# Two slabs of the gate's u moved in front of the opening norm, and the second block's opening norm moved two steps later

## The chip, the cores and the metric

The kernel runs on one core of one Trainium2 chip. The metric is the device time of one execution in microseconds (us), as the median of several runs. TensorE (PE) multiplies matrices into PSUM; VectorE (DVE), ScalarE (ACT) and GpSimd (POOL) do the elementwise work; SyncE (SP) issues most of the DMAs. In the rows of the profile, PEld is TensorE's loading of weights.

## What is computed

Two transformer blocks stand one behind the other over one sequence of 512 tokens and 1024 features. The change touches the mixer of the first block and the entry into the second. Cut to that, the reference is:

```
# first block
a = rmsnorm(h, ln_pre_mix)
q, k, v, u, z = split(a @ w_in)
attn = dilated_attention(q, k, v)
u, z = gelu(u), gelu(z)                       # the spatial gate, 4 groups of 128 features
z = layernorm(z, ln_g, ln_b)                  # within each group
sgu = u * (einsum('gij,bnjgc->bnigc', wm, zc) + b_s)
h = h + rmsnorm(concat(rmsnorm(attn), rmsnorm(sgu)) @ w_out)
...                                           # feed-forward, then a sigmoid gate on h
# second block
h = rms_norm(x, norm_mix) * (1 + sc1) + sh1
q, k, v = split(h @ w_in)                     # stick-breaking attention
...
```

A norm here is a factor per token (one over the root of the mean square) and a gain per feature. The kernel puts the gain into the operand in advance and the factor on the product behind it, so that a projection can start before the norm's factor is known.

## The kernel before, in words

Activations are kept feature by token: eight tiles `X` of 128 features by 512 tokens. Every product of two fp32 numbers is made of three passes: each operand is split into a high part (`whi`, `hh`, cast by ACT) and the rest (`wlo`, `hl`, subtracted by DVE), and `mm3` (line 95 issues every matmul) runs low weights, high weights, and high weights with the low activations. A **slab** is 128 output features by 512 tokens: 8 steps over the features times 3 passes, 24 matmuls of 128x512 into one PSUM bank. `tokmajor` makes a product token by feature instead, in four banks at once: 96 matmuls. One `unit` (line 101) loads 512 KB of weights on SP's queue and splits them into two pairs `whi`, `wlo`; there are four buffers for raw weights and seven each for `whi` and `wlo`, so a cast waits until TensorE is through with the pair seven places back.

PSUM has three banks `mm`, two banks `sc`, one bank `po` and a pair `tt`.

A norm over the features has two halves. `norm_cols` (line 235) multiplies the summed squares by a column of ones on TensorE (rows `tt<-ones1k,acc`), DVE adds epsilon (`ms`, line 241) and GpSimd takes the power -1/2 (`rc`, line 243). `norm_rows` (line 246) spreads `rc` over all partitions by TensorE (rows `tt<-ident,rc`), and DVE copies the result to `R` (line 258). `stats` is one behind the other. The sum of squares is made by ACT (`sq`, line 209) and added up on GpSimd or DVE (`acc`, line 204).

`mixer_a` (line 354) opens the first block. The product for z comes first, token by feature, in the three `mm` banks and `po`; then `stats` gives `rc0` and `R0`; then the product for v takes the same four banks, which the four gelus of z (line 403, scaled by `rc0`) must have left. The shift of the gate (`RB`, line 419, from eight small matmuls `sc<-wmT,lnb` and `sc<-bsr,onesr`) and the layer norm of z follow. Then, for each of the four groups, one slab for u, its product with `R0` on DVE, its gelu on ACT, four small matmuls `sc<-wmT,z` and the gating.

`enter` (line 848) opens each half of the second block's layers, with `b` from 0 to 3: four slabs (two `mm` banks, one `sc`, `po`) run over the unnormed activations `xd`, step by step over the features, each step 12 matmuls in the four banks. Between the steps stand the norm's columns and, one step later, its rows. Behind it `operand` (lines 879 to 881) makes the eight normed activations out of `R`, and `slab` (line 863) puts `R` on the four products, which frees their banks. After `enter(b=0)`, `mixer_sb` runs the product for v, token by feature, in the three `mm` banks and one `sc`.

The order in which instructions stand on an engine is not that of the code: the tile framework's scheduler sets it when the kernel is built. On an engine each instruction waits for the one before it.

Of the kernel before, what the change touches and what calls it, by code (L numbers as in the profile page):

```python
# [8 lines left out]
F32 = mybir.dt.float32  # L9
F32R = mybir.dt.float32r  # L10
BF16 = mybir.dt.bfloat16
AF = mybir.ActivationFunctionType
# [3 lines left out]
P = 128  # L16
S = 512
NB = S // P
D = 1024
KD = D // P  # L20
# [45 lines left out]
class K:  # L66
# [287 lines left out]
    def mixer_a(self, X, raw):  # L354
        tc, nc, a = self.tc, self.nc, self.a
        xs = []
# [7 lines left out]
        with ExitStack() as ctx:  # L364
            mp = ctx.enter_context(self.homes("mixa", [f"m{p}{i}" for p in "hl" for i in range(8)]))
            gctx = ctx.enter_context(ExitStack())
            pm2 = gctx.enter_context(tc.tile_pool(name="gate", bufs=1))
            w0 = a["w_in"]
# [9 lines left out]
            acc = None  # L378
            for k in range(KD):
                acc = self.add_square(acc, X[k])  # L380
            rc0, R0 = self.stats(acc, self.ones1k)

            pv = self.four()
            self.tokmajor(pv, [w0[8 + i] for i in range(4)], xs)
# [40 lines left out]

            sacc, ms = None, [None] * 8
            for g in range(4):
                pu = self.mm_ps()
                self.slabs([pu], [self.unit(w0[4 + g])], xs)
                u = self.t(pm2, [P, S], F32, "u", bufs=2)  # L430
                nc.vector.tensor_mul(u, pu, R0)
                nc.scalar.activation(u, u, AF.Gelu_apprx_tanh)
                pmx = self.sc_ps()
                for tb in range(NB):
                    self.matmul(pmx[:, tb * P:(tb + 1) * P], zt[tb][:, g * P:(g + 1) * P], wmT[:, g, :],
                                     start=True, stop=True)
                m = self.t(pm2, [P, S], F32, "m", bufs=2)
                nc.vector.scalar_tensor_tensor(m.rearrange("p (b i) -> p b i", b=NB),
                                               pmx.rearrange("p (b i) -> p b i", b=NB), self.col("sgu_ln_g"),
                                               RB[:, g:g + 1, :].to_broadcast([P, NB, P]), op0=ALU.mult, op1=ALU.add)  # L440
                nc.vector.tensor_mul(u, u, m)
                ms[4 + g] = self.split_scaled(u, self.col("sgu_out_norm", g), 4 + g, "m", mp)
                sacc = self.add_square(sacc, u, mp, "sacc")
# [7 lines left out]
            aacc, ks = [None], {}  # L451
# [66 lines left out]
            pss = []  # L518
# [329 lines left out]
    def enter(self, X, b, ws):  # L848

        nc = self.nc
        pss = [self.bank("mm"), self.bank("mm"), self.bank("sc"), self.bank("po")]
        w = self.units(ws)
        self.slabs(pss, w, self.xd, ks=range(0, 2))
        rc = self.norm_cols(self.acc, self.ones1k)
        self.slabs(pss, w, self.xd, ks=range(2, 3))
        R = self.norm_rows(rc)
        self.slabs(pss, w, self.xd, ks=range(3, KD))

        def slab(i, out=None, raw=False):
            u = self.t(self.sp, [P, S], F32, "sq", bufs=2) if out is None else out
            nc.vector.tensor_mul(u, pss[i], R)
            if raw:
                return u, self.bsh[b][:, i:i + 1]
            nc.scalar.activation(u, u, AF.Identity, bias=self.bsh[b][:, i:i + 1])
            return u

        mod, sh = self.mod[b // 2], 24 * (b % 2)

        def operand(pool, tag):

            xs = []
            for k in range(KD):
                hi = self.t(self.xp, [P, S], F32R, f"hh{k}", bufs=1)
                lo = self.t(self.xp, [P, S], F32R, f"hl{k}", bufs=1)
                f = self.t(pool, [P, S], F32, tag(k), bufs=1)
                shift = mod[:, sh + k:sh + k + 1]
                nc.vector.scalar_tensor_tensor(f, X[k], self.A[b][:, k:k + 1], R, op0=ALU.mult, op1=ALU.mult)  # L879
                nc.scalar.activation(hi, f, AF.Identity, bias=shift)  # L880
                nc.vector.scalar_tensor_tensor(lo, f, shift, hi.bitcast(F32), op0=ALU.add, op1=ALU.subtract)  # L881
                xs.append((hi, lo))
            return xs

        return slab, operand
# [522 lines left out]
```

## Time and profile before

| | |
|---|---|
| median of 3 runs | 1922.7 us (1921.9 to 1925.36) |
| the profiled execution's own time | 1926.12 us |
| its span, first to last instruction | 1924.4 us |
| TensorE busy | 1877.1 us, 98% of the span |
| VectorE, ScalarE, GpSimd busy | 1289.8, 897.7, 372.8 us |
| mean granted TensorE clock | 0.987 of full speed |

The times of runs are taken without the profiler; all views below are of the one profiled execution. Times in them count from the start of its span. A granted clock of 1.00 is 2.4 GHz, one of 0.50 is 1.2 GHz.

### The profile page before, as it was taken

How to read it: one execution, taken by the hardware profiler on the slowest of the kernel's cores; microseconds unless marked ns; L12 is line 12 of the kernel's file. 1: busy time of each engine (PE TensorE's matmuls, PEld its weight loads, DVE VectorE, ACT ScalarE, POOL GpSimd, SP SyncE). 2: the span in 40 equal slices, each digit the busy share in tenths (PEclk: the TensorE clock that was granted, in tenths of full speed). 3: DMA queues.
4: the chain of work that ended last, by engine and by line, in shares of the span. 5: the costliest groups of instructions: out<-in, count | busy, mean ns of one | idle time of the engine just before them, and what ended most of it. 6: DMA issues, size and time to landing. Idle time of an engine off the chain costs nothing.

```text
span 1924.4 us, 24081 instructions
## 1 busy us (share of the span) xinstructions
PE 1877.1 (98%) x8610; PEld 1508.7 (78%) x8610; DVE 1289.8 (67%) x2354; ACT 897.7 (47%) x1664; POOL 372.8 (19%) x348
## 2 busy tenths in 40 slices
PE   7999799999999999999999999999999999999999
PEld 5887678888887787777888888887666788888887
DVE  7686775556446666886878875568977677666431
ACT  5365433323323555554544443336489755444321
POOL 3020431111000302332111110003454211111000
PEclk8999899999999999999999999999999999999999
DMA  5232155555464233222266554633222123223331
GB/s 184 88 90 88 44 165 186 192 189 175 153 210 164 88 120 90 78 64 81 99 215 198 188 186 151 208 122 104 72 72 67 35 99 117 91 99 96 96 114 45
DMA packets 70382, 236.93 MB, mean 123 GB/s; under 512 B 8086, under 2 KB 8678, under 8 KB 70263
## 3 DMA queue, kind: packets, MB, share of 16 engines
q1 hardware_dynamic: 69556, 234.47, 37.8%
q8 instruction: 67, 1.10, 0.2%
q10 hardware_dynamic: 578, 0.85, 0.1%
q14 instruction: 53, 0.43, 0.1%
q0 software_dynamic: 128, 0.08, 0.0%
HBM read 226.87 MB, written 2.21 MB: 119 GB/s over the span
## 4 chain that ended last, share of the span: by engine, by line
PE 77%; DVE 6%; issue 2%; ACT 1%; POOL 0%; POOLq 0%; DVEq 0%; ACTq 0%
PE mm L95 45%; PE sc L95 26%; PE po L95 3%; PE tt L98 2%; PE tt L95 1%; DVE isc L1123 1%; DVE m L1122 1%; DVE hl L276 0%; DVE g L768 0%; DVE hl L881 0%; DVE v L1060 0%; DVE rst L223 0%; DVE isc L1103 0%; DVE q L879 0%; DVE wlo L113 0%
## 5 line engine op out<-in xcount | busy, mean ns | idle before, releaser
L113 DVE TENSOR_TENSOR wlo<-raw,whi 128x512 fp32r<-128x512 f32 (+1 forms) x518 | 381.1, 744 | 203.6 <-ACT whi L112 199.0
L112 ACT CAST whi<-raw 128x512 fp32r<-128x512 f32 (+1 forms) x550 | 326.8, 607 | 405.7 <-PE mm L95 236.4
L95 PE MATMUL mm<-hh,wlo 128*128 128x512 f32 (+1 forms) x1000 | 406.4, 406 | 3.5 <-ACT hh L275 3.5
L95 PE MATMUL mm<-hl,whi 128*128 128x512 f32 x1032 | 401.2, 392 | 0.0
L95 PE MATMUL mm<-hh,whi 128*128 128x512 f32 (+1 forms) x1000 | 392.0, 392 | 0.0
L95 PEld LDWEIGHTS mm<-hl,whi 128*128 128x128 f32 x1032 | 194.5, 188 | 42.3
L95 PEld LDWEIGHTS mm<-hh,wlo 128*128 128x128 f32 (+1 forms) x1000 | 189.3, 189 | 47.9 <-issue 8.5
L796 DVE CUSTOM_DVE_ANT_0 ada<-ada,bc 128x1024 f32<-128x1024 f32 x112 | 138.2, 1234 | 127.6 <-DMA ada<-in_ada_w 101.4
L95 PEld LDWEIGHTS mm<-hh,whi 128*128 128x128 f32 (+1 forms) x1000 | 189.1, 189 | 36.8 <-issue 1.1
L204 POOL TENSOR_TENSOR acc<-acc,sq 128x512 f32<-128x512 f32 x53 | 89.5, 1688 | 394.8 <-ACT sq L209 387.2
L95 PE MATMUL sc<-hh,wlo 128*128 128x512 f32 x416 | 162.8, 391 | 0.0
L95 PE MATMUL sc<-hl,whi 128*128 128x512 f32 x416 | 162.6, 391 | 0.0
L95 PE MATMUL sc<-hh,whi 128*128 128x512 f32 x416 | 162.5, 391 | 0.0
L95 PE MATMUL mm<-Hh,wlo 128*128 128x512 f32 x364 | 143.3, 394 | 0.0
L95 PE MATMUL mm<-Hh,whi 128*128 128x512 f32 x364 | 143.0, 393 | 0.0
L95 PE MATMUL mm<-Hl,whi 128*128 128x512 f32 x364 | 143.0, 393 | 0.0
L1034 POOL TENSOR_TENSOR g<-g,u 128x512 f32<-128x512 f32 x44 | 62.8, 1428 | 413.1 <-DVE u L1030 341.4
L266 ACT CAST Hh<-g 128x512 fp32r<-128x512 f32 x66 | 41.0, 622 | 164.2 <-POOL g L720 101.4
L95 PEld LDWEIGHTS sc<-hh,wlo 128*128 128x128 f32 x416 | 78.7, 189 | 16.3
L95 PEld LDWEIGHTS sc<-hl,whi 128*128 128x128 f32 x416 | 78.5, 189 | 16.5
L95 PEld LDWEIGHTS sc<-hh,whi 128*128 128x128 f32 x416 | 78.6, 189 | 16.3
L95 PE MATMUL sc<-Hh,wlo 128*128 128x512 f32 x220 | 86.7, 394 | 0.0
(370 smaller groups left out, 3328.8 us busy)
## 6 DMA issues: line engine op xcount, KB each, us to landing
ada<-in_ada_w SPq DMA_DIRECT2D x96, 512.0 KB, 3.9
raw<-in_ffn_w_up SPq DMA_DIRECT2D x88, 512.0 KB, 3.3
raw<-in_w_gate_up SPq DMA_DIRECT2D x44, 512.0 KB, 4.2
raw<-in_ffn_w_down SPq DMA_DIRECT2D x32, 512.0 KB, 3.6
raw<-in_sb_w_in SPq DMA_DIRECT2D x24, 512.0 KB, 3.2
raw<-in_dsa_w_in SPq DMA_DIRECT2D x21, 512.0 KB, 3.4
raw<-in_w_in SPq DMA_DIRECT2D x19, 512.0 KB, 3.3
raw<-in_w_down SPq DMA_DIRECT2D x16, 512.0 KB, 4.3
```

Of the source, the lines that this page charges most:

```text
L95: self.queue(self.nc.tensor.matmul(*args, **kw))
L98: self.queue(self.nc.tensor.transpose(*args))
L112: nc.scalar.copy(hi[:, :w], raw[:, c:c + w])
L113: (eng or nc.vector).tensor_sub(lo[:, :w], raw[:, c:c + w], hi[:, :w].bitcast(F32))
L204: (eng or self.nc.gpsimd).tensor_add(acc, acc, self.square(src))
L266: self.nc.scalar.copy(hi, src)
L796: nc.vector.tensor_tensor_reduce(raw, raw, row, scale=1.0, scalar=0.0, op0=ALU.mult, op1=ALU.add, accum_out=out))
L1034: nc.gpsimd.tensor_mul(g, g, u)
L1122: nc.vector.max(m8, work[qb][:, :L])
L1123: nc.vector.match_replace(work[qb][:, :L], m8, work[qb][:, :L], SENT)
```

## The change

In `mixer_a` the slabs of the first two groups of u are multiplied right behind z, into the two `sc` banks. The norm's columns come behind the first of the two slabs, the norm's rows behind the second. The product with `R0` and the gelu of these two groups follow at once, in front of v; the loop over the groups makes only the slabs of groups 2 and 3. In `enter`, for `b` = 0, the columns come behind the fourth step in place of the second, and the rows behind the fifth in place of the third; for `b` = 1 to 3 nothing changes. No instruction is added or removed on any engine.

```diff
@@ mixer_a
             for k in range(KD):
                 acc = self.add_square(acc, X[k])
-            rc0, R0 = self.stats(acc, self.ones1k)
+
+            pus = []
+            for g in range(2):
+                pus.append(self.sc_ps())
+                self.slabs(pus[-1:], [self.unit(w0[4 + g])], xs)
+                if g == 0:
+                    rc0 = self.norm_cols(acc, self.ones1k)
+            R0 = self.norm_rows(rc0)
+            us = []
+
+            def gated(g, pu):
+                u = self.t(pm2, [P, S], F32, "u", bufs=2)
+                nc.vector.tensor_mul(u, pu, R0)
+                nc.scalar.activation(u, u, AF.Gelu_apprx_tanh)
+                us.append(u)
+
+            for g in range(2):
+                gated(g, pus[g])
 
             pv = self.four()
             self.tokmajor(pv, [w0[8 + i] for i in range(4)], xs)
@@
             for g in range(4):
-                pu = self.mm_ps()
-                self.slabs([pu], [self.unit(w0[4 + g])], xs)
-                u = self.t(pm2, [P, S], F32, "u", bufs=2)
-                nc.vector.tensor_mul(u, pu, R0)
-                nc.scalar.activation(u, u, AF.Gelu_apprx_tanh)
+                if g > 1:
+                    pu = self.mm_ps()
+                    self.slabs([pu], [self.unit(w0[4 + g])], xs)
+                    gated(g, pu)
+                u = us[g]
                 pmx = self.sc_ps()
@@ enter
         w = self.units(ws)
-        self.slabs(pss, w, self.xd, ks=range(0, 2))
+        k = 2 if b else 4
+        self.slabs(pss, w, self.xd, ks=range(0, k))
         rc = self.norm_cols(self.acc, self.ones1k)
-        self.slabs(pss, w, self.xd, ks=range(2, 3))
+        self.slabs(pss, w, self.xd, ks=range(k, k + 1))
         R = self.norm_rows(rc)
-        self.slabs(pss, w, self.xd, ks=range(3, KD))
+        self.slabs(pss, w, self.xd, ks=range(k + 1, KD))
```

How the order on the engines moves, at three places. First TensorE behind the product for z (the last matmul into `po`), before and then with the change; a row with x4 is four matmuls.

```order
L95 MATMUL po_133<-wlo_274,hh_64_290 128x512
L95 MATMUL tt_334<-ones1k_101,acc_311 128x1 x4
L95 MATMUL sc_580<-wmT_498,lnb_505 128x128
L95 MATMUL sc_580<-bsr_501,onesr_503 128x128
L95 MATMUL tt_343<-ident_96,rc_341 128x128 x4
...
L95 MATMUL mm_350<-whi_356,hl_32_135 128x512
```

```order
L95 MATMUL po_133<-wlo_274,hh_64_290 128x512
L95 MATMUL sc_334<-hh_31_134,wlo_338 128x512
...
L95 MATMUL tt_369<-ones1k_101,acc_311 128x1 x4
L95 MATMUL sc_378<-hh_31_134,wlo_382 128x512
...
L95 MATMUL tt_413<-ident_96,rc_376 128x128 x4
L95 MATMUL mm_426<-whi_432,hl_32_135 128x512
```

A slab of 24 matmuls now stands in front of the columns (`tt_369`), another between them and the rows (`tt_413`), and v (`mm_426`) follows the rows directly; the eight small matmuls for `RB` stand behind v.

Second, VectorE in the same stretch, before and then with the change (`lbase` and `lt` belong to the attention's bias, made early; the `wlo` are those of v, and with the change they are v's first five).

```order
L643 TENSOR_TENSOR lbase_837<-lbase_837,lt_194_838 128x512
L113 TENSOR_TENSOR wlo_425<-raw_422,whi_424 128x512
L113 TENSOR_TENSOR wlo_429<-raw_422,whi_428 128x512
L241 TENSOR_SCALAR ms_339<-tt_334 128x4
L113 TENSOR_TENSOR wlo_459<-raw_456,whi_458 128x512
L258 COPY R_348<-tt_343 128x512
```

```order
L660 TENSOR_TENSOR lbase_837<-lbase_837,lt_194_838 128x512
L113 TENSOR_TENSOR wlo_433<-raw_430,whi_432 128x512
L113 TENSOR_TENSOR wlo_437<-raw_430,whi_436 128x512
L113 TENSOR_TENSOR wlo_467<-raw_464,whi_466 128x512
L113 TENSOR_TENSOR wlo_471<-raw_464,whi_470 128x512
L241 TENSOR_SCALAR ms_374<-tt_369 128x4
L113 TENSOR_TENSOR wlo_501<-raw_498,whi_500 128x512
```

`ms` now stands behind four subtractions of v's weights in place of two.

Third, VectorE in `enter(b=0)`, before and then with the change (`hl_1330` and `acc` end the first block; `mh` and `hl` are `operand`'s, `wlo_5694` the last weights of the four slabs).

```order
L204 TENSOR_TENSOR acc_5426<-acc_5426,sq_5642 128x512
L241 TENSOR_SCALAR ms_5726<-tt_5721 128x4
L258 COPY R_5747<-tt_5742 128x512
L879 SCALAR_TENSOR_TENSOR mh_1373_5828<-X_1_81,A_19_113,R_5747 128x512
L137 TENSOR_TENSOR wlo_5694<-raw_5663,whi_5693 128x512
```

```order
L204 TENSOR_TENSOR acc_5426<-acc_5426,sq_5642 128x512
L137 TENSOR_TENSOR wlo_5694<-raw_5663,whi_5693 128x512
L113 TENSOR_TENSOR wlo_5915<-raw_5912,whi_5914 128x512
L113 TENSOR_TENSOR wlo_5919<-raw_5912,whi_5918 128x512
L241 TENSOR_SCALAR ms_5750<-tt_5745 128x4
L113 TENSOR_TENSOR wlo_5949<-raw_5946,whi_5948 128x512
L258 COPY R_5771<-tt_5766 128x512
L897 SCALAR_TENSOR_TENSOR mh_1373_5828<-X_1_81,A_19_113,R_5771 128x512
```

Three subtractions of weights have come in front of `ms`, one between `ms` and `R`. Behind `R`, 15 of the 16 operations of `operand` still stand in front of the first product that frees a bank (`sq<-mm`). On TensorE v's first matmuls are reordered for it: 15 matmuls into the free banks `mm_5908` and `sc_5911` come before the first into `mm_5909`, where before there were three.

## Rows read from the trace of the kernel before

**Rows 1.** The page, busy us (share of the span) and instructions per engine.

```profile
PE 1877.1 (98%) x8610; PEld 1508.7 (78%) x8610; DVE 1289.8 (67%) x2354; ACT 897.7 (47%) x1664; POOL 372.8 (19%) x348
```

**Rows 2.** Waits of TensorE: who for whom, us in total, times, longest us.

```profile
PE tt L95 <- POOL rc L243: 9.4, 4, 5.2
PE tt L95 <- DVE acc L204: 8.7, 3, 5.4
```

**Rows 3.** Timeline of TensorE, opening norm: start us, us, form, xcount, idle before.

```profile
31.58 0.95 PE L95 MATMUL tt<-ones1k,acc 128*128 128x1 f32 x8
32.39 0.47 PE L95 MATMUL sc<-wmT,lnb 128*128 128x128 f32 x2
32.78 0.48 PE L95 MATMUL sc<-bsr,onesr 1*128 1x128 f32 x2
38.45 2.07 PE L95 MATMUL tt<-ident,rc 128*128 128x128 f32 x8 [5.18 <-POOL rc L243]
40.31 0.63 PE L95 MATMUL sc<-wmT,lnb 128*128 128x128 f32 x2
...
44.49 0.80 PE L95 MATMUL mm<-whi,hl 128*128 128x512 f32 x1
...
48.34 0.40 PE L95 MATMUL po<-whi,hl 128*128 128x512 f32 x1
```

**Rows 4.** Windows: stretch, its us, busy us (instructions) per engine, PEclk, DMA.

```profile
38.50:48.30 9.80, 9.80 (x29) 7.68 (x30) 4.19 (x27) 2.93 (x5) 0.00 (x0) 0.51 0.10 38
```

**Rows 5.** The chain that ended last, in order of time, a piece at full clock.

```profile
264.17 10.88 PE mm L95 x48
```

**Rows 6.** Timeline of DVE, POOL and ACT, opening norm.

```profile
35.12 1.70 DVE L113 TENSOR_TENSOR wlo<-raw,whi 128x512 fp32r<-128x512 f32 x2
...
36.98 1.41 POOL L243 TENSOR_TENSOR rc<-ms,mhalf 128x4 f32<-128x4 f32 x1 [0.70 <-DVE ms L241]
...
32.19 1.28 ACT L403 ACT_TABLE_LOAD   x1
38.43 1.84 ACT L403 ACTIVATE z<-mm,rc 128x512 f32<-128x512 f32 x3 [4.96 <-POOL rc L243]
```

**Rows 7.** DMA issues of the page: xcount, KB each, median us to landing.

```profile
raw<-in_w_in SPq DMA_DIRECT2D x19, 512.0 KB, 3.3
```

**Rows 8.** Timeline of TensorE, the second block's opening norm.

```profile
666.17 0.39 PE L95 MATMUL po<-hl,whi 128*128 128x512 f32 x1
669.22 1.69 PE L95 MATMUL tt<-ones1k,acc 128*128 128x1 f32 x8 [2.66 <-DVE acc L204]
670.77 0.77 PE L95 MATMUL mm<-hh,wlo 128*128 128x512 f32 x1
...
676.03 1.14 PE L95 MATMUL tt<-ident,rc 128*128 128x128 f32 x8
676.93 0.48 PE L95 MATMUL mm<-hh,wlo 128*128 128x512 f32 x1
...
690.62 0.39 PE L95 MATMUL mm<-whi,hl 128*128 128x512 f32 x1
```

**Rows 9.** Windows, the stretch behind that wait.

```profile
669.30:676.90 7.60, 7.60 (x28) 6.44 (x28) 0.16 (x1) 0.00 (x0) 1.03 (x1) 0.55 0.05 17
```

**Rows 10.** Timeline of DVE and POOL, the second block's opening norm.

```profile
668.39 0.68 DVE L204 TENSOR_TENSOR acc<-acc,sq 128x512 f32<-128x512 f32 x1
...
677.21 0.69 DVE L258 COPY R<-tt 128x512 f32<-128x512 f32 x1 [6.10 <-PE tt L95]
...
681.87 0.75 DVE L879 SCALAR_TENSOR_TENSOR mh<-X,A,R 128x512 f32<-128x512 f32 x1
682.53 0.75 DVE L881 SCALAR_TENSOR_TENSOR hl<-mh,mod,hh 128x512 fp32r<-128x512 f32 x1
...
689.70 1.28 DVE L863 TENSOR_TENSOR sq<-mm,R 128x512 f32<-128x512 f32 x2
...
671.19 1.03 POOL L243 TENSOR_TENSOR rc<-ms,mhalf 128x4 f32<-128x4 f32 x1 [3.64 <-DVE ms L241]
```

## The prediction

> **What bounds the kernel now.** I read the page first: TensorE is busy 98% of the span [rows 1], so a change pays where TensorE stands still or runs at a lower clock, and nowhere else. Next the waits of TensorE: among the longest are those of the norms, for `rc` (9.4 us in 4 waits, the longest 5.2) and for `acc` (8.7 us in 3) [rows 2]. The timeline gives their places. The 5.18 us wait for `rc` is the opening norm of the first block [rows 3]; one of the waits for `acc`, 2.66 us, stands in front of the second block's columns [rows 8]. The change goes to these two places. Last the windows, because a wait here costs more than itself: behind the first wait the granted clock is 0.51 for 9.8 us [rows 4], behind the second 0.55 for 7.6 us [rows 9], that is the lower of the two levels, 1.2 GHz, for all or most of the stretch. TensorE had stood still before each. At the upper level 48 matmuls take 10.88 us, 0.2267 us each [rows 5].
>
> **The opening norm of the first block: what is lost.** Behind z's product the columns start at 31.58, and v's matmuls run at the upper level again from 48.34, after nine of them at the lower [rows 3]. These 16.76 us hold:
> - the columns, 31.58 to 32.39, 0.81 us, at the upper level;
> - one pair of the `RB` matmuls, in the shadow of the wait; its first half takes 0.39 us (32.39 to 32.78), so a pair about 0.78;
> - the wait, 5.18;
> - the rows, 38.45 to 40.31, 1.86; rows at the upper level take 0.90 (676.03 to 676.93) [rows 8], so 0.96 is lost;
> - three pairs of `RB`, 40.31 to 44.49, 4.18 against 3 x 0.78 = 2.34, so 1.84 is lost;
> - nine matmuls of v, 44.49 to 48.34, 3.85 against 9 x 0.2267 = 2.04, so 1.81 is lost.
>
> The loss is 5.18 + 0.96 + 1.84 + 1.81 = 9.8 us. The slabs that move cost nothing by themselves: the same 48 matmuls run earlier, and no longer after v.
>
> **Does it come back?** Only if TensorE finds everything ready in the new order. I follow it from 31.58 at 0.2267 us a matmul. The first u slab ends at 37.02, the columns at 37.83, the second slab at 43.27, the rows at 44.17; there v starts.
> - `ms` now stands behind four subtractions of v's weights. VectorE reaches the first at 35.12; two took 1.70 there [rows 6], the other two take, at 0.85, as much, to 38.5. The casts they need wait for weight buffers; the last is free when TensorE is through the first half of the first slab, 34.3. The columns are done at 37.83, so `ms` runs at 38.5, and GpSimd's power (1.41 us [rows 6]) ends by 40.2. The rows are due at 43.27: 3 us in hand.
> - v needs z's four banks. Their gelus need `rc` at 40.2 and the table load of 1.28 us [rows 6] behind a cast that can start at 37.02, so the table is there by 39. Three gelus took 1.84 [rows 6]; a cast and the fourth follow, and the first bank is free by 41, the fourth by 43.5; v wants the first at 44.17 and the fourth nine matmuls later, at 46.2. This is the cover that shrinks: before, the six small `RB` matmuls of 4.18 us also stood between `rc` and v, now only the rows' 0.90.
> - The two slabs hold both `sc` banks until `R0` is there. The next to want one is `RB`, and it has moved behind v, over 20 us later.
> - On SP's queue the two loads of u's weights pass four of v's. Each is 512 KB, 3.3 us to landing [rows 7], the same size as what it passes, and the buffers free at the same rate, a unit each 24 matmuls (5.44 us). The first unit is the one that was cast for v before, at the same moment. No cost.
> - Behind v come eight `RB` matmuls, 3.1 us at the upper level, already in the sum. ACT's and DVE's work on u is only moved, to a stretch in which TensorE is the one waited for.
>
> I take 9.8 us, with no new wait. The bounds are 5.18, the wait alone (a run whose clock had not been lowered would get no more back), and 9.8.
>
> **The second block's opening norm: what is lost.** The last matmul before the columns begins at 666.17, so TensorE is through with it at 666.40. The columns begin only at 669.22, 2.82 us later, because the last square is added by VectorE at 668.39 for 0.68 us, to 669.07 [rows 8, 10]. At the lower clock the columns then take 1.55 (669.22 to 670.77) for 0.81, and twelve matmuls 5.26 (670.77 to 676.03) for 2.72. The loss is 2.82 + 0.74 + 2.54 = 6.1 us.
>
> With two more steps, 24 matmuls and 5.44 us, in front, the columns are reached at 671.84. `acc` has been ready for 2.8 us, so that wait goes whole. The columns end at 672.65 and the next step at 675.37. Between them `ms` runs, and `rc` took 1.03 us on GpSimd [rows 10], perhaps the 1.41 of the first norm: done by 674.6, so the rows are not late. `R` is copied 1.18 us after the rows begin (676.03 to 677.21), at 676.55, only 0.7 us earlier than before. TensorE, though, ends the four slabs at 671.84 + 0.81 + 2.72 + 0.90 + 36 x 0.2267 = 684.4, where before v began at 690.62 [rows 8].
>
> **What is late next** is VectorE: it gains 0.7 us where TensorE gains 6. After `R` (0.69) 15 operations of `operand` at 0.66 us (681.87 to 682.53) lead to 687.1, and the two products that free `mm` banks end at 687.8 and 688.4 [rows 10]. TensorE has 15 matmuls for the free banks, 3.4 us, to 687.8. So about 0.2 us of wait is new. At 0.75 us an operation, the busy time of the row, it would be 1.3; at the measured pace and with TensorE a little later, nothing. I take 0.2, since the pace is measured in the same chain.
>
> **The sum.** 9.8 + 6.1 - 0.2 = 15.7 us. The profiled execution took 1926.12 us and would take 1910.4. That execution stands 3.4 us above the median of the runs, so on the median the forecast is 1922.7 - 15.7 = **1907.0 us**, 0.8% less. Everything behind moves forward with it: the work after each place depends on TensorE's progress, whose weight loads follow it.
>
> **Where a rule is weighed.** The rows show the lower clock behind both waits of this one execution, for 9.8 and 7.6 us. The Trainium skill, "TensorE: Matmul & The Clock Gate", section "What's actually happening", says that the clock is lowered unless the engine is active, and that the watch runs free of the kernel, so that the number of slow matmuls differs from run to run. No second profile here shows that. By that rule part of the clock terms could be missing in other executions, and the gain would lie between the two waits alone and the whole sum.
>
> **Rivals.**
> - *Only the waits come back.* If in the timed runs the clock stayed up behind these waits, there is no slow stretch to save. Then 5.18 + 2.82 = 8.0 us, less 0.2: 1914.9 us. For it: the profiled execution is slower than each of the timed ones. Against it: both waits, even the shorter one, were followed by the lower clock. Chance 0.09.
> - *VectorE becomes the bound in the second block.* If `operand`'s chain is so late that TensorE waits for its `mm` bank as long as it did for `acc` (2.66), the clock falls again, and the 6.1 us are given back: 1922.7 - 9.8 = 1912.9 us. For it: VectorE gains 0.7 us only. Against it: the estimated wait is 0.2 and its bound 1.3. Chance 0.09.
> - *v waits for z's gelus in the first block.* With a wait as long as the old one, the 9.8 us are given back: 1922.7 - 5.9 = 1916.8 us. For it: `RB` no longer covers them. Against it: almost 3 us in hand. Chance 0.04.
> - *Slower.* The same place: `rc` so late that TensorE waits at the rows with both `sc` banks held and v not startable. With a clock loss of 4.6 us (0.96 + 1.84 + 1.81) on top, the first block's gain is gone at a wait of 9.8 - 4.6 = 5.2 us, the whole gain at 11, and from 15 us on the kernel is over 0.2% slower: 1926.6 or more. It would take `ms` behind a subtraction whose buffer only v frees; the order shows it behind buffers freed by the first slab. Chance 0.02.
>
> **How the numbers follow.** The forecast has 0.73, and two of the first three rivals at once 0.03. A measurement of this kernel can tell about 0.2%, 3.8 us, from no change. Faster by more than that: the forecast and each of the first three rivals alone, 0.73 + 0.09 + 0.09 + 0.04 = 0.95. Within: two rivals at once, 0.03. Slower: 0.02. The range goes down 4 us from the forecast, since the runs spread by 3.5 us and the profiled run had 3.4 us more than the median, and up to 1914.9, which takes in the first two rivals: 1903 to 1915.
>
> **What would show it.** In the changed profile: no wait of TensorE for `rc` or `acc` between 30 and 70 us, and a granted clock of 1.00 from 11 us to the end of v; v starting near 44.2 and ending near 66; the second block's columns right behind the fourth step, without a wait, the rows one step later at 1.00; v of the second block starting about 16 us earlier in the span than 690.62, and at most a short wait for `mm`. A wait of over 2 us with a lower clock behind it, at v in either block, would prove me wrong.

## The result and the profile after

The kernel after the change takes 1909.86 us (median of 4 runs, 1906.52 to 1911.36), the kernel before, in runs between these, 1924.0 us (4 runs, 1921.9 to 1925.36). The ratio is 0.9923, 95% interval 0.9911 to 0.9936: 14 us less. The prediction said 1907.0 and a range of 1903 to 1915. The profiled execution of the kernel after took 1911.36 us with a span of 1909.7, against 1926.12 and 1924.4 before: 14.8 us less (14.7 in the span), where the sum of the prediction said 15.7. The mean granted clock rose from 0.987 to 0.992.

The page's line of TensorE, which answers to [rows 1]: TensorE stands still or crawls less, and does the same 8610 matmuls.

```profile
PE 1871.8 (98%) x8610; PEld 1505.3 (79%) x8610; DVE 1289.6 (68%) x2354; ACT 897.2 (47%) x1664; POOL 373.4 (20%) x348
```

The waits of TensorE for the two halves of the norms (us in total, times, longest), against [rows 2]: the longest wait for `rc`, 5.2, is gone, and one of the three for `acc`.

```profile
PE tt L95 <- DVE acc L204: 5.7, 2, 5.4
PE tt L95 <- POOL rc L243: 4.3, 3, 1.7
```

The timeline of TensorE at the two places, against [rows 3, 8]. In the first block the first u slab begins at 31.79, the columns stand behind it at 37.23, the rows behind the second slab at 43.57, v begins at 44.38 and its end is followed by `RB` at 66.26. None of these rows has an idle time in brackets behind it. In the second block the columns begin at 661.97 and the rows at 665.59, each at the upper level (0.95 and 1.05 where [rows 8] has 1.69 and 1.14), and v at 674.68 in place of 690.62.

```profile
31.79 0.39 PE L95 MATMUL sc<-hh,wlo 128*128 128x512 f32 x1
...
37.23 0.95 PE L95 MATMUL tt<-ones1k,acc 128*128 128x1 f32 x8
...
43.57 1.05 PE L95 MATMUL tt<-ident,rc 128*128 128x128 f32 x8
44.38 0.48 PE L95 MATMUL mm<-whi,hl 128*128 128x512 f32 x1
...
66.26 0.38 PE L95 MATMUL sc<-wmT,lnb 128*128 128x128 f32 x2
...
661.97 0.95 PE L95 MATMUL tt<-ones1k,acc 128*128 128x1 f32 x8
...
665.59 1.05 PE L95 MATMUL tt<-ident,rc 128*128 128x128 f32 x8
...
674.68 0.39 PE L95 MATMUL mm<-whi,hl 128*128 128x512 f32 x1
...
678.10 0.50 PE L95 MATMUL mm<-whi,hl 128*128 128x512 f32 x1
```

The windows over both places (stretch, its us, busy us of the engines, then PEclk, DMA share, GB/s), against [rows 4, 9]. Where the granted clock was 0.51 and 0.55 behind the waits, it is 1.00 in every stretch, and TensorE is busy for all of it.

```profile
31.60:44.00 12.40, 12.40 (x62) 10.49 (x61) 10.61 (x35) 6.32 (x10) 2.43 (x2) 1.00 0.55 176
44.00:66.00 22.00, 22.00 (x101) 18.30 (x100) 14.92 (x52) 7.48 (x13) 0.00 (x0) 1.00 0.28 95
...
668.00:675.00 7.00, 7.00 (x33) 5.79 (x32) 7.00 (x12) 4.88 (x8) 0.00 (x0) 1.00 0.00 0
```

The timeline of VectorE, GpSimd and ScalarE, against [rows 6, 10]. First block: `ms` runs at 38.22 behind four subtractions, GpSimd's power ends at 39.89, the gelus of z's four banks run from 39.92 to 42.87. Second block: the last square is added at 658.50, the copy of `R` begins at 666.68, and the two products that free `mm` banks begin at 677.37.

```profile
35.35 2.91 DVE L113 TENSOR_TENSOR wlo<-raw,whi 128x512 fp32r<-128x512 f32 x4
38.22 0.16 DVE L241 TENSOR_SCALAR ms<-tt 128x4 f32<-128x4 f32 x1
...
38.46 1.43 POOL L243 TENSOR_TENSOR rc<-ms,mhalf 128x4 f32<-128x4 f32 x1 [1.95 <-DVE ms L241]
...
39.92 1.27 ACT L420 ACTIVATE z<-mm,rc 128x512 f32<-128x512 f32 x2 [0.57 <-POOL rc L243]
...
42.17 0.70 ACT L420 ACTIVATE z<-po,rc 128x512 f32<-128x512 f32 x1
...
658.50 0.68 DVE L204 TENSOR_TENSOR acc<-acc,sq 128x512 f32<-128x512 f32 x1
...
663.03 0.69 DVE L113 TENSOR_TENSOR wlo<-raw,whi 128x512 fp32r<-128x512 f32 x1
...
663.20 1.41 POOL L243 TENSOR_TENSOR rc<-ms,mhalf 128x4 f32<-128x4 f32 x1 [5.54 <-DVE ms L241]
...
666.68 0.69 DVE L258 COPY R<-tt 128x512 f32<-128x512 f32 x1 [2.95 <-PE tt L95]
...
677.37 1.27 DVE L881 TENSOR_TENSOR sq<-mm,R 128x512 f32<-128x512 f32 x2
```

**Where the time went.** The same matmul can be found in both traces, and the difference of its start says what has been won up to there. I use two stretches that hold the same matmuls in both kernels. The *gate*: from the last matmul of z's product (31.35 before, 31.57 after) to the first of the third u slab (80.73, 71.29), 49.38 us before and 39.72 after: 9.66 won. The *entry*: from the last matmul that stands ahead of the columns before the change (666.17) to v's first (690.62), 24.45 us; after, 24 more matmuls of 0.2267 us stand ahead of the columns, so the stretch is 674.68 - 661.75 + 5.44 = 18.37: 6.08 won. Together 15.74. The whole difference is 14.8, so about 1 us was lost elsewhere; the last experiment shows where.

### The profile page after: what moved, and what is told of

The parts are those of the page before. It is cut to its first block, busy times and chain, and to the rows that moved or that the text cites. A ratio compares the mean times of both kernels' runs of the same rounds, so it can differ in the third digit from the quotient of the medians.

```text
span 1909.7 us, 24071 instructions
## 1 busy us (share of the span) xinstructions
PE 1871.8 (98%) x8610; PEld 1505.3 (79%) x8610; DVE 1289.6 (68%) x2354; ACT 897.2 (47%) x1664; POOL 373.4 (20%) x348
## 4 chain that ended last, share of the span: by engine, by line
PE 79%; DVE 5%; issue 1%; ACT 1%; POOL 0%; POOLq 0%; ACTq 0%; DVEq 0%
PE mm L95 47%; PE sc L95 26%; PE po L95 3%; PE tt L98 2%; PE tt L95 1%; DVE isc L1141 1%; DVE m L1140 1%; DVE hl L899 0%; DVE v L1078 0%; DVE rst L223 0%; DVE isc L1121 0%; DVE q L897 0%; ACT A L671 0%; DVE acc L986 0%; DVE rst L224 0%
## 5 line engine op out<-in xcount | busy, mean ns | idle before, releaser
L95 PE MATMUL mm<-hh,wlo 128*128 128x512 f32 (+1 forms) x984 | 399.6, 406 | 3.5 <-ACT hh L275 3.5
L95 PE MATMUL mm<-hl,whi 128*128 128x512 f32 (+1 forms) x1016 | 394.9, 392 | 0.0
L95 PE MATMUL mm<-hh,whi 128*128 128x512 f32 (+1 forms) x984 | 385.3, 392 | 0.0
L95 PEld LDWEIGHTS mm<-hl,whi 128*128 128x128 f32 (+1 forms) x1016 | 191.4, 188 | 41.3
L95 PE MATMUL sc<-hh,wlo 128*128 128x512 f32 x432 | 168.8, 391 | 0.0
L95 PE MATMUL sc<-hh,whi 128*128 128x512 f32 x432 | 168.4, 390 | 0.0
L95 PE MATMUL sc<-hl,whi 128*128 128x512 f32 x432 | 168.3, 390 | 0.0
```

Of the source, the lines that this page charges most:

```text
L95: self.queue(self.nc.tensor.matmul(*args, **kw))
```

## The experiments

All times below are medians; each ratio is to the kernel before, run on the same chip between the others (medians 1924.64, 1924.65, 1924.55 and 1925.52 in the four comparisons of experiments).

| kernel | us (runs) | ratio, 95% interval | gate, us | entry, us |
|---|---|---|---|---|
| before | 1924.0 (4) | 1 | 49.38 | 24.45 |
| after | 1909.86 (4) | 0.9923, 0.9911 to 0.9936 | 39.72 | 18.37 |
| gate_only | 1915.43 (5) | 0.9946, 0.9931 to 0.9962 | 40.67 | 22.88 |
| entry_only | 1920.83 (12) | 0.9977, 0.9964 to 0.999 | 49.80 | 18.37 |
| entry_filled | 1923.88 (12) | 0.9997, 0.9984 to 1.0011 | 49.96 | 21.21 |
| one_slab | 1909.76 (6) | 0.9923, 0.9906 to 0.9939 | 40.34 | 18.37 |
| entry_three | 1909.41 (5) | 0.9924, 0.991 to 0.9939 | 39.72 | 18.57 |
| entry_six | 1914.55 (6) | 0.995, 0.9933 to 0.9966 | 39.72 | 19.34, then 1.93 |
| ffn_slab | 1906.55 (4) | 0.9904, 0.9888 to 0.9921 | 39.72 | 18.37 |
| ffn_filled | 1911.42 (6) | 0.993, 0.9913 to 0.9947 | 39.73 | 18.37 |
| before_again | 1923.66 (11) | 0.999, 0.9979 to 1.0002 | 49.89 | 22.86 |
| after_again | 1908.45 (6) | 0.9919, 0.9903 to 0.9935 | 39.72 | 18.38 |
| ffn_filled2 | 1908.61 (5) | 0.9913, 0.9897 to 0.9928 | 40.93 | 18.37 |
| ffn_slab_again | 1907.66 (4) | 0.9908, 0.9894 to 0.9922 | 39.72 | 18.37 |

The last two columns are the two stretches in the profiled execution of each kernel, worked out from starts of matmuls as above (for entry_three 12 and for entry_six 48 more matmuls ahead of the columns; for entry_filled from the matmul in front of the scrap).

**One part alone.** gate_only is the kernel after with the second block as before:

```diff
-        k = 2 if b else 4
+        k = 2
```

> The first part of the change alone: two slabs of u in front of v, the second block's entry as before. My theory (wait plus slow clock behind it): 9.8 us less than before, about 1914; in the profile no wait for rc in front of v and a clock of 1.00 there, but the 2.66 us wait for acc in the second block still stands. Rival (only the wait comes back): 5.2 us less, about 1919. Rival (the two parts depend on each other): anything whose sum with the run of the second part alone is not about 15.

entry_only is the kernel before with only the second block changed:

```diff
-        self.slabs(pss, w, self.xd, ks=range(0, 2))
+        k = 2 if b else 4
+        self.slabs(pss, w, self.xd, ks=range(0, k))
...
-        self.slabs(pss, w, self.xd, ks=range(2, 3))
+        self.slabs(pss, w, self.xd, ks=range(k, k + 1))
...
-        self.slabs(pss, w, self.xd, ks=range(3, KD))
+        self.slabs(pss, w, self.xd, ks=range(k + 1, KD))
```

> The second part alone: only the second block's opening norm comes two steps later. My theory: 5.9 us less than before, about 1918, with v of the second block starting about 6 us earlier against the columns than before. Rival (only the wait comes back): 2.7 us less, about 1921. Rival (VectorE is the bound there): no change.

Measured: 1915.43 against 1924.64 for gate_only, 9.2 us less (by the interval 7.3 to 13.3), as expected. entry_only is 3.8 us less (1.9 to 6.9), less than the 5.9 expected, though the interval holds it. Its trace has no wait and no lower clock at the place, and its stretch is 18.37 us as in the kernel after. So the change did there all that it does in the kernel after; what it is compared with can differ, and gate_only, which has the old entry, shows it. The timeline of TensorE in gate_only:

```profile
660.78 1.02 PE L95 MATMUL tt<-ones1k,acc 128*128 128x1 f32 x8 [2.65 <-DVE acc L204]
661.66 0.48 PE L95 MATMUL mm<-hh,wlo 128*128 128x512 f32 x1
...
662.85 0.63 PE L95 MATMUL mm<-hh,whi 128*128 128x512 f32 x1
...
666.09 1.05 PE L95 MATMUL tt<-ident,rc 128*128 128x128 f32 x8
```

The wait is the same 2.65 us, but the columns run at the upper level (1.02 us, where [rows 8] has 1.69), the lower clock comes later, and it is over before the rows. The old stretch is 22.88 us here and was 24.45 in the first profile: the change wins 4.5 us against the one and 6.1 against the other. The two gains in time add up to 13.0 us, the whole change won 14.1: with intervals as wide as these, nothing that speaks for the third expectation, parts that depend on each other.

**The clock by itself.** entry_filled is the kernel before with twelve matmuls into a scrap tile in front of the second block's columns; the wait for `acc` stays, and TensorE works in it.

```diff
+        if b == 0:
+            self.idle(12, self.xd[1])
         rc = self.norm_cols(self.acc, self.ones1k)
```

> The kernel before, with twelve matmuls into a scrap bank in front of the second block's columns, in the place of the 2.66 us wait for acc. They give no work that is needed, so the wait stays, filled. My theory: TensorE does not stand still, the clock stays at its upper level, and the columns, the step behind them and the rows run at it: 3.3 us less than before (0.74 + 2.54), about 1920.5, and a window of the 7 us behind the columns at a clock of 1.00. Rival (the slow stretch has another cause than the standstill): the window stays near 0.55, and the time stays the same or becomes up to 0.5 us longer.

The timeline of TensorE has the scrap, the columns and the rows, all at the upper level:

```profile
665.67 2.88 PE L95 MATMUL tt<-hh 128*128 128x512 f32 x12
668.62 1.05 PE L95 MATMUL tt<-ones1k,acc 128*128 128x1 f32 x8
...
672.13 1.05 PE L95 MATMUL tt<-ident,rc 128*128 128x128 f32 x8
```

The stretch is 21.21 us, 3.2 less than in the first profile of before and 1.65 less than in gate_only. The clock did what the theory said, the 3.3 us did not show in the time: it is not to be told from no change (0.9984 to 1.0011), which a gain of 1.65 us could hide in and one of 3.3 hardly. One profile with the clock up would prove little where the clock is loose. But all three profiles in which TensorE stands still here (before, before_again, gate_only) have the lower clock between the columns and v, and none of the other eleven has it.

**How much cover is needed.** one_slab puts the columns right behind z, one slab between columns and rows, and the other behind the rows:

```diff
+            rc0 = self.norm_cols(acc, self.ones1k)
             for g in range(2):
...
                 if g == 0:
-                    rc0 = self.norm_cols(acc, self.ones1k)
-            R0 = self.norm_rows(rc0)
+                    R0 = self.norm_rows(rc0)
```

> The changed kernel with one slab as cover in place of two: columns at once behind z, then the first slab of u, the rows, the second slab, then v. The first slab ends 6.3 us after the columns begin; rc came 6.8 us after them before. My theory: a wait of about 0.5 to 1 us in front of the rows, without a lower clock, so about 0.5 to 1 us longer than the changed kernel, not to be told from it in time (1910 to 1911). Rival (both slabs are needed as cover): a wait of over 2 us with a lower clock behind it, 4 us or more longer than the changed kernel, 1914 or more.

The timeline of TensorE:

```profile
31.11 0.95 PE L95 MATMUL tt<-ones1k,acc 128*128 128x1 f32 x8
37.99 1.16 PE L95 MATMUL tt<-ident,rc 128*128 128x128 f32 x8 [0.37 <-POOL rc L243]
```

One slab of 5.4 us leaves a wait of 0.37 us with no lower clock behind it, and the time is that of the kernel after, 1909.76. The gate is 0.6 us longer in its trace (40.34 for 39.72), about as expected. The second slab only gives margin.

entry_three and entry_six move the second block's columns to the third and the sixth step:

```diff
-        k = 2 if b else 4
+        k = 3 if b == 0 else 2
```

> After's kernel with the columns of the second block's opening norm after three steps instead of four. Theory (moving them matters only by covering VectorE's sums, which are 2.7 us late after two steps; one step of 12 matmuls is 2.72 us): TensorE reaches the columns just as the sums end, waits 0 to 0.3 us, no lower clock behind, and the time is that of the kernel after the change within 0.5 us (about 1910). Rival (the columns must stand well behind the sums, since rc's chain on VectorE and GpSimd is as long as a step): TensorE waits at the rows, 1 us or more, and about 2 us are lost (1912).

> After's kernel with the same columns after six steps. Theory (VectorE's chain from the norm's R over the operands mh, ml, hl to the freed bank has only some 0.1 us in hand after four steps, and its R now comes 5.4 us later): v waits about 1 us for its first operand and some 2 us for a free mm bank, with the lower clock behind them 5 to 7 us over the kernel after the change (about 1916). Rival (TensorE alone bounds this place, VectorE has slack): within 0.5 us of the kernel after the change (about 1910).

entry_three took 1909.41 us, that is no difference to the kernel after, and its stretch is 0.2 us longer: the rival, 2 us lost at the rows, is out. entry_six took 1914.55, 4.7 us more. The timeline of TensorE there shows the two waits in front of v and in v; the lower clock follows the second (0.63 us per matmul from 684.67):

```profile
675.94 0.50 PE L95 MATMUL mm<-whi,hl 128*128 128x512 f32 x1 [0.81 <-DVE hl L899]
...
683.16 0.50 PE L95 MATMUL mm<-whi,hl 128*128 128x512 f32 x1 [1.93 <-DVE sq L881]
...
684.67 0.63 PE L95 MATMUL mm<-whi,hl 128*128 128x512 f32 x1
```

So the theory holds: VectorE's chain out of `R` is next in line, and four steps leave it little more than nothing. Both sides of the choice are measured: two steps leave a wait for the sums, six a wait for VectorE, three and four leave 0.2 us at most.

**The same edit in another place.** ffn_slab takes the kernel after and puts a slab of `w_gate_up` between columns and rows of a norm in the first feed-forward part, where the rows had waited 1.74 us for `rc` at 248.04:

```diff
-            _, R = self.stats(acc, self.ones1k)
+            rc = self.norm_cols(acc, self.ones1k)
+            ps.append(self.bank("sc"))
+            self.slabs(ps[-1:], [self.unit(a["w_gate_up"][4])], xs)
+            R = self.norm_rows(rc)
...
-                        ps.append(self.any_ps())
-                        self.slabs(ps[-1:], [self.unit(a["w_gate_up"][2 * n + j])], xs)
+                        if 2 * n + j > 4:
+                            ps.append(self.any_ps())
+                            self.slabs(ps[-1:], [self.unit(a["w_gate_up"][2 * n + j])], xs)
```

> After's kernel with one more norm split in the same way: the one of the first feed-forward part whose rows waited 1.74 us for GpSimd at 248.04; one slab of w_gate_up (24 matmuls, 5.4 us) is put between its columns and its rows. Theory (what counts is TensorE's wait and the lower clock behind it, wherever it stands): the wait of 1.74 us, the 0.9 to 1.0 us that the rows take longer at the lower clock and some 1.1 us of slow matmuls behind them go, 3 to 4 us less than the kernel after the change (about 1906.5). Rival (the lower clock here was owed to the 1.16 us wait ahead of it and comes back, or the slab only moves the wait): 0 to 1.7 us less (1908 to 1910).

The columns stand at 245.14, the rows at 251.48 without a wait in front of them:

```profile
251.48 1.05 PE L95 MATMUL tt<-ident,rc 128*128 128x128 f32 x8
```

From these columns to those of the next such norm it is 343.48 us (245.14 to 588.62) here and 345.04 in ffn_slab_again (246.04 to 591.08), against 347.24 in the kernel after (245.36 to 592.60) and 346.81 in after_again (245.81 to 592.62). So 1.8 to 3.8 us are won in the traces, and the 3 to 4 of the theory only with the first profile of ffn_slab; in the second the next columns wait 1.48 us for `acc`, in the first 0.02. The medians, 1906.55 and 1907.66 in the two times it ran, are 1 to 3 us under those of the kernel after; the intervals of the ratios overlap, so the runs don't prove the gain. They are the lowest two here.

ffn_filled adds scrap matmuls to ffn_slab in the three waits of the norm ahead of that one:

```diff
+        self.idle(FILL[0], X[0])
+        rc = self.norm_cols(macc, self.ones1k)
+        self.idle(FILL[1], X[0])
+        R = self.norm_rows(rc, "bc")
+        self.idle(FILL[2], X[0])
```

> ffn_slab with matmuls into a scrap tile (20, 4 and 9 of 128x128, some 0.24 us each) standing in the three waits of the first norm of the first feed-forward part (5.36, 1.35 and 3.47 us at 205 to 224 in the trace of the kernel after the change). They compute nothing; the waits are chains on other engines and stay. Theory (behind a standstill of several us the clock is lowered, and work that keeps TensorE going keeps it up): columns 0.9 us, rows 1.0 us and the ten slow matmuls behind them 2.3 us quicker, 4.2 us less than ffn_slab (about 1902). Rival (the clock is lowered whatever stands in the wait, or the scrap overruns the wait by as much): no less than ffn_slab, or up to 1 us more.

It took 1911.42 us, more than ffn_slab: neither theory. The timeline of VectorE shows why; the scrap read `X`, which VectorE was about to write, and VectorE waited for the scrap to end.

```profile
220.72 1.29 DVE L644 TENSOR_TENSOR X<-X,hh 128x512 f32<-128x512 f32 x2 [1.74 <-PE tt L96]
```

From these columns to the next it is 37.29 us (211.09 to 248.38), in ffn_slab 34.16. That is 3.1 of the 4.9 us; where the rest of it arose stays open. The lower clock came all the same, from about 213.7, behind waits of 0.92 and 0.26 us that the scrap had left.

ffn_filled2 lets the scrap read a constant:

```diff
-                self.matmul(scrap[:, :P], self.ident, x[:, :P], start=True, stop=True)
+                self.matmul(scrap[:, :P], self.ident, self.ident, start=True, stop=True)
```

> ffn_filled with the scrap matmuls reading the constant identity alone instead of X, which VectorE is about to overwrite in this place (in ffn_filled VectorE waited 1.74 us for the scrap before it could write X, and everything behind came 2.5 us late), and 22 in place of 20 in front of the columns. Theory (what TensorE executes in its waits keeps the clock up, and the loss in ffn_filled was that wait of VectorE's): no wait of VectorE for TensorE there, the first matmul behind the norm at 217 to 219 instead of 219.70, and 2 to 4 us less than ffn_slab (1902.5 to 1904.5). Rival (the clock falls in this place whatever TensorE does, as it did in ffn_filled at 213.7 behind a wait of only 0.92 and 0.26 us): the rows and the matmuls behind are at the lower clock again, and at most 1 us is won (1905.5 to 1907).

> ffn_slab unchanged, beside ffn_filled2 on the same chip and as a second profile: the slab behind the columns again without a wait at the rows and with no lower clock between 240 and 262 us; 1905 to 1908.

In ffn_filled2 the clock stays up; these are its windows:

```profile
217.00:224.00 7.00, 6.59 (x37) 5.65 (x38) 7.00 (x11) 3.62 (x6) 2.74 (x1) 1.00 0.00 0
224.00:236.00 12.00, 9.06 (x40) 6.89 (x38) 12.00 (x13) 6.53 (x11) 8.89 (x6) 1.00 0.14 45
236.00:246.00 10.00, 10.00 (x37) 8.13 (x38) 6.49 (x8) 3.00 (x5) 2.71 (x2) 0.83 0.47 157
```

And these rows of its timeline of TensorE say what it was worth:

```profile
212.39 1.02 PE L96 MATMUL tt<-ones1k,acc 128*128 128x1 f32 x8 [0.46 <-DVE acc L211]
...
219.58 0.49 PE L96 MATMUL mm<-hh,wlo 128*128 128x512 f32 x1 [0.41 <-ACT hh L282]
...
235.97 0.49 PE L96 MATMUL po<-hh,wlo 128*128 128x512 f32 x1 [2.94 <-DVE wlo L138]
...
246.53 0.95 PE L96 MATMUL tt<-ones1k,acc 128*128 128x1 f32 x8
```

From the columns to the next matmul of the part it is 7.19 us, in ffn_slab 8.72 (210.98 to 219.70). But VectorE is busy for 12.00 of the 12.00 us from 224 to 236, so TensorE only comes earlier to a wait: 2.94 us for `wlo`, where ffn_slab has 1.33, and then the lower clock. From these columns to the next it is 34.14 us, in ffn_slab 34.16 (210.98 to 245.14). Both expectations on the time fail: the clock was won back, as the theory had it, and nothing came of it, because another engine paces that stretch. At the next norm this execution waits 4.31 us for `acc` (594.32), where ffn_slab waited 0.02 and ffn_slab_again 1.48; what makes that wait so loose, these runs don't show. ffn_slab_again came as expected: no wait at the rows, a clock of 1.00 from 240 to 262, 1907.66 us.

**The two kernels once more.** before_again and after_again are the two kernels unchanged, profiled a second time.

> The kernel before, unchanged, profiled a second time. Theory (waits repeat, the stretch of lower clock behind a wait of 1 to 2 us does not): the two gate waits (1.29 or so and 5.18 us at 38 us, 2.66 us at 669 us) and their lower clock come again, the waits of 1.16 us near 606 us and 2.02 us near 1315 us come again within 0.1 us, and at one or both of them the lower clock starts earlier or later, or fails to come, so that the time between two like matmuls there differs by 0.5 us or more from the first profile. Rival (the lower clock follows from the waits alone): the windows of 50 us show the same clock as in the first profile, within 0.01, everywhere.

> The kernel after, unchanged, profiled a second time. Theory: against the second profile of before, the matmuls behind the gate stand 9.7 us earlier and those behind the second block's opening norm 6.1 us more than those in front of it, within 0.3 us, whatever the clock does elsewhere; median 1907 to 1911 and 14 to 16 us under before. Rival (the two gains are as loose as the rest of the clock): one of the two differs by over 0.5 us from the first pair of profiles.

The spans are 1919.7 and 1906.5: 13.2 us. The timeline of TensorE in before_again, at the entry:

```profile
666.55 1.08 PE L95 MATMUL tt<-ones1k,acc 128*128 128x1 f32 x8 [2.65 <-DVE acc L204]
667.49 0.78 PE L95 MATMUL mm<-hh,wlo 128*128 128x512 f32 x1
...
670.62 0.48 PE L95 MATMUL sc<-hh,whi 128*128 128x512 f32 x1
...
671.86 1.05 PE L95 MATMUL tt<-ident,rc 128*128 128x128 f32 x8
...
1310.42 0.41 PE L98 MATMUL tt<-ident,Th 8*128 8x8 f32 x4 [2.01 <-ACT Th L1083]
```

The waits come again (5.21 for 5.18 us, 2.65 for 2.66), the lower clock at the entry does not: it begins here as the columns end and takes some eight matmuls, where it took the columns and twelve matmuls in the first profile. The gate wins 49.89 - 39.72 = 10.17 us in this pair, the entry 22.86 - 18.38 = 4.48. My theory, 6.1 within 0.3 at the entry, is out, and the rival is right there: that gain is as loose as the clock. At the gate it is firmer: 49.38, 49.80, 49.89 and 49.96 us in four profiles of the old order, and 39.72 in seven of the nine with the order of the kernel after, so 9.7 to 10.2 won; in the other two, gate_only and ffn_filled2, a stretch of lower clock falls into its end, and 1 us or more is lost again.

Of the expectations for before_again neither holds as a whole. The theory looked for a difference near 606 and 1315, and there neither profile of the kernel before has the lower clock (1.00 from 600 to 650 and from 1300 to 1350 in both). The rival, the same clock everywhere, fails at the entry: 0.93 from 650 to 700 in the first profile, 0.97 in the second. What the theory says of waits is shown by the kernel after, in a place that the change doesn't touch: both its profiles have the same wait for `Th`, and only one has the lower clock behind it. First the kernel after, then after_again:

```profile
1298.92 0.41 PE L98 MATMUL tt<-ident,Th 8*128 8x8 f32 x4 [2.02 <-ACT Th L1101]
1299.26 0.63 PE L95 MATMUL mm<-hl,whi 128*128 128x512 f32 x1
```

```profile
1297.37 0.41 PE L98 MATMUL tt<-ident,Th 8*128 8x8 f32 x4 [2.02 <-ACT Th L1101]
1297.70 0.50 PE L95 MATMUL mm<-hl,whi 128*128 128x512 f32 x1
```

This is where the 1 us of the first pair went. Between the gate and the entry the kernel after won 1.9 us more: 0.6 by a shorter wait for `wlo` (1.16 for 1.80 us, at 246 in the trace before), the rest mostly by less of the lower clock behind it. It lost 1.5 at 595.39, where eight matmuls run at the lower level behind a wait of 1.16 us and in the kernel before, behind the same wait, none. Behind the wait for `Th` it lost another 1.5, of which 0.2 came back near 1400. In the second pair most of the 1.5 us that are missing (10.17 + 4.48 - 13.2) were lost near 250, where the lower clock followed the rows in after_again and not in before_again.

## Why the prediction was right

**The gate, 9.8 us.** Measured 9.7 and 10.2 in two pairs, 9.2 in time. By terms: the wait of 5.18 is gone; the rows take 43.57 to 44.38, 0.81, where I priced 0.90; v starts at 44.38, where I had 44.17, of which 0.21 is that the stretch itself began later; the eight `RB` matmuls take 3.2 (66.26 to 69.48) for 3.1. The chain that had to be in time was: `ms` at 38.22 for 38.5, `rc` done at 39.89 for 40.2, the last of z's banks free at 42.87 for 43.5.

**The entry, 6.1 us.** The wait of 2.82 is gone in every kernel with the new order. The clock's part, 0.74 + 2.54 = 3.28, was right for the execution it was read from (6.08 won in all) and is not what the kernel pays each time: 1.66 in before_again (4.48 - 2.82) and 1.69 in gate_only. This is the term that was mis-sized, and the step was to take the 0.55 of [rows 9] for a property of the wait. The other end of it, the wait alone, was kept as a rival. Here the sentence from the Trainium skill, "TensorE: Matmul & The Clock Gate", section "What's actually happening", that the watch on the engine's activity runs free of the kernel and that the count of matmuls at the lower clock varies by run, has its evidence: the page tells it of a kernel's start, and the second profile shows it in mid-kernel, 24.45 and 22.86 us behind the same wait. By that rule the gain lies anywhere from the two waits alone, 8.0 us, to the whole sum; the medians say 14 to 16.

**The new wait, 0.2 us.** v's sixteenth matmul, the first that needs a freed `mm` bank, starts at 678.10 where the fifteenth began at 677.85, and the one behind it at 678.43: 0.58 us for two steps in place of 0.45. So it is 0.13 us, and entry_six, which makes the same chain 5.4 us later, turns it into 0.81 + 1.93 us and a lower clock. That VectorE would be the next to be late, and how near it is, was right. `R` came 0.7 us earlier in the order of things, as predicted: 677.21 - 666.68 = 10.53, of which 9.87 had been won before.

**`rc` on GpSimd** was read as 1.03 us "perhaps 1.41". It took 1.41: a subtraction on VectorE with two inputs now runs beside it, 663.03 to 663.72, where VectorE had been idle. Without one it takes 1.03 at this place, in before, before_again, gate_only, entry_filled, entry_three and entry_six; in all eight profiles with the subtraction beside it, it takes 1.41. The Trainium skill, "GPSIMD Engine Reference", section "1. Specifications", says that GpSimd shares its interfaces to SBUF with VectorE, whose instructions with two SBUF inputs contend with it; the traces agree, at 0.4 us. It cost nothing, as the rows came later still.

**The forecast of the time**, 1907.0, is 2.9 under the median: 1.3 because the kernel before took 1924.0 with the fourth run in place of the 1922.7 shown, and 1.6 in the gain (14.1 for 15.7), which the second comparison with 16.1 (1924.55 to 1908.45) doesn't repeat. Of the rivals, "only the waits come back" is out for the gate, where all four profiles of the old order have the lower clock behind the wait, and half true for the entry; "VectorE becomes the bound" is two steps further on; at the gate `rc` is done 3.7 us before the rows begin (39.89 to 43.57), where the prediction worked out 3, and the last of z's banks is free before v begins at all (42.87 to 44.38).

**Open.** gate_only has a stretch of lower clock from about 72, inside the gate, and ffn_filled2 one from about 69.5. The order of the instructions up to there is the same on all four engines as in the kernel after, so the order does not make it. A wait for a weight's low part does not either: gate_only has one of 0.36 us at 28.37, ffn_slab_again one of 0.38 at 27.30 without a lower clock behind it, and ffn_filled2 none. What differs between these executions and the others stays open.

## What to carry to other kernels

When a norm, or any chain over other engines, makes TensorE wait, work that needs nothing from it and whose result has a free bank to stay in is worth the wait and the lower clock behind it; read from the trace how long the chain is and put just that much in front, since each step more shortens the time of the engine that works on the chain's result. Price the wait from the trace, and the clock behind it as a range from nothing to what one profile shows, until a second profile has been read. Where another engine is busy for the whole of the next stretch, keeping TensorE's clock up buys only a longer wait at its end.

## What was not expected of the hardware

The same wait is followed by the lower clock in one execution and not in another: 2.02 us at the wait for `Th`, the lower level at once in one profile of the kernel after and the upper throughout in the other; 2.65 us at the entry, behind it the lower level for the columns and twelve matmuls (24.45 us for the stretch) or for some eight matmuls (22.86 and 22.88).

And the clock fell where TensorE stood still nowhere that the trace shows. These are windows of gate_only; TensorE is busy for all of each, with small matmuls of 128x128 from 68 to 73.9, and no row from 29 on has an idle time:

```profile
70.00:72.00 2.00, 2.00 (x14) 1.64 (x14) 0.00 (x0) 0.59 (x1) 0.00 (x0) 0.99 0.00 0
72.00:74.00 2.00, 2.00 (x13) 2.00 (x11) 1.27 (x2) 0.00 (x0) 0.00 (x0) 0.50 0.00 0
74.00:76.00 2.00, 2.00 (x8) 1.62 (x7) 1.85 (x4) 1.24 (x2) 0.00 (x0) 0.66 0.00 0
```

And this is one of ffn_filled2, with the same small matmuls:

```profile
70.00:72.00 2.00, 2.00 (x12) 2.00 (x11) 1.24 (x2) 0.00 (x0) 0.00 (x0) 0.50 0.00 0
```

The kernel after runs them at 66.26 to 71.29 with the clock at 1.00, and so do the other six profiles with this order. Why the clock fell in two and not in the others, these runs don't show.
